# Constants made on GpSimd, columns turned by TensorE, and late constants moved off the weight queue, in a two-layer hybrid decoder

## The chip, the cores and the metric

The kernel runs on one core of a Trainium2 chip. The metric is device time in microseconds (us) of one execution. Three runs of the kernel before took 957.54, 958.25 and 959.33 us; the median, 958.25 us, is the time to compare with. One more execution was profiled; its span, from the first to the last instruction, is 955.9 us.

Engine names: TensorE (PE in the rows; PEld is its weight load), VectorE (DVE), ScalarE (ACT), GpSimd (POOL) and SyncE (SP, which issues most DMAs).

## The reference

Two layers of a decoder trunk, 256 tokens of width 1024, all in float32. What touches the change:

```python
for layer in range(2):
    h = rms_norm(x, norm_mix_pre[layer])
    m = mixer_block(h, positions, w_in[layer], conv_w[layer], ret_gn_w[layer], gla_w_a2[layer],
                    gla_b_a[layer], gla_gn_w[layer], w_branch_a[layer], w_branch_b[layer],
                    w_branch_c[layer], w_out[layer])
    x = x + rms_norm(m, norm_mix_post[layer])
    h = rms_norm(x, norm_ffn_pre[layer])
    f = (silu(h @ w_gate) * (h @ w_up)) @ w_down
    x = x + rms_norm(f, norm_ffn_post[layer])
```

`mixer_block` projects h with w_in (1024 x 8208, the first weights to be used) and cuts the result into the inputs of three branches and their gates: a short causal convolution of three taps (`conv_w`), a retention with rotary positions (cos and sin of position times frequency, masks of powers of a decay), and gated linear attention (GLA), whose decay comes from the data through a 16-column projection and `gla_w_a2`, `gla_b_a`. The branches' results are normalized per head (`ret_gn_w`, `gla_gn_w`), gated, projected and summed.

## The kernel before

**Products.** Float32 products are made of three products of two float32r parts: each operand is split into hi (a cast on ScalarE, `whi`, L206) and lo (the rest, a subtraction on VectorE, `wlo`, L208). TensorE then does hi hi, hi lo and lo hi into one bank (`piece`, L290). The activations are split in the same way into `hT0hi`, `hT0lo` for the first 128 tokens (tile 0) and `hT1hi`, `hT1lo` for the second (tile 1).

**The weight stream.** `Weights` lists all weights in the order of use, cut in units of at most 128 x 1024 numbers, 512 KB. A unit is loaded by SP into one of four buffers `raw` (L192), split into one of eight slots, and multiplied with both tiles. A load waits for a free `raw`, which the subtraction of an earlier unit gives back; a split waits for a slot, which TensorE's last product of an earlier unit gives back. In the first layer the units are, in order: 0 to 4 the GLA q and k (512 columns), 5 and 6 half of the GLA output gate (256 columns), 7 to 9 the other half with the 16 decay columns (272 columns), 10 to 13 the retention q (`rq`), 14 to 17 its k (`rk`), 18 to 21 its v, and so on.

**What sets the order.** TensorE's and SP's programs run in the order that the code writes, in which `Order` interleaves side tasks (generators that yield a time or a condition) with the stream of products. ScalarE, VectorE and GpSimd get an order from the tile scheduler, which follows priorities (`urgent()`, `tc.high_priority`) and `issue_after` bounds. Each engine runs its instructions strictly in that order, and so do the DMA queues' issuing engines: an instruction that waits holds up all behind it.

**The start.** TensorE multiplies zeros (`warm`) until data is there. `first_norm` transposes x through `ident` (L296), multiplies by the norm's weight column `wcol` (L539) and splits; the norm's factor per token is applied later, when a bank is drained (`drain`, L577, with `rs` as scale). `first_rstd` makes these factors: a sum of squares on ScalarE (L547), then on GpSimd an addition (L548) and a power (L370).

**Constants.** One table `consts` in DRAM holds the identity, two decay masks for the retention (`cst`, C_DD and C_DO), `mlev` (nine 128x128 matrices that sum log decays within blocks of 1 to 64 tokens), `lmask` (seven 128x64 masks) and the rotary frequencies. SP loads them: the identity first of all (L317), `freq` and `posi` (L322, L323) ahead of the first weights, `lmask` and the decay masks (L364, L365) behind unit 7; GpSimd's queue loads `mlev` (L552). At each layer's start SP loads the two head-norm weights broadcast to all partitions (`gnw`, L564), the decay projection (`wa`, L569, L570) and the conv taps as columns (`cw`, L573, three DMAs).

**The two places that drain.** The bank of the 272-column block is drained by four instructions (L577, into `ga` and `long`); the next products of tile 1 need these banks. `ga` is transposed and copied to `gaT` (L658), and `wa` times `gaT` (names `ac<-wa,gaT`) is in TensorE's program right behind.

## Time and profile before

| | |
|---|---|
| median of three runs | 958.25 us (957.54 to 959.33) |
| span of the profiled execution | 955.9 us |
| mean granted TensorE clock | 0.986 |
| TensorE busy | 927.0 us (97%) |
| VectorE busy | 578.2 us (60%) |
| ScalarE busy | 461.6 us (48%) |
| GpSimd busy | 74.4 us (8%) |
| DMA | 166.55 MB, mean 174 GB/s |

Busy shares are means over the whole span. In a timeline row the bracket at the end gives the idle time of the engine just ahead of the instruction and what ended it. `x3` is a count. A granted clock of 1.00 is 2.4 GHz, 0.5 is 1.2 GHz. The executions' own time is some 2 us above the span, which begins with the first instruction.

### The profile page before, as it was taken

How to read it: one execution, taken by the hardware profiler on the slowest of the kernel's cores; microseconds unless marked ns; L12 is line 12 of the kernel's file. 1: busy time of each engine (PE TensorE's matmuls, PEld its weight loads, DVE VectorE, ACT ScalarE, POOL GpSimd, SP SyncE). 2: the span in 40 equal slices, each digit the busy share in tenths (PEclk: the TensorE clock that was granted, in tenths of full speed). 3: DMA queues.
4: the chain of work that ended last, by engine and by line, in shares of the span. 5: the costliest groups of instructions: out<-in, count | busy, mean ns of one | idle time of the engine just before them, and what ended most of it. 6: DMA issues, size and time to landing. Idle time of an engine off the chain costs nothing.

```text
span 955.9 us, 12593 instructions
## 1 busy us (share of the span) xinstructions
PE 927.0 (97%) x4828; PEld 755.9 (79%) x4828; DVE 578.2 (60%) x830; ACT 461.6 (48%) x609; POOL 74.4 (8%) x83
## 2 busy tenths in 40 slices
PE   7779999999999999999989999999999999999997
PEld 5757888888888888888977778888888888888895
DVE  5569858654467655455475976775456765455443
ACT  4465364544436644444456545454444564444431
POOL 1002220101000000000010233010020000000000
PEclk8889999999999999999999999999999999999999
DMA  9994558877635766655779546697765467566521
GB/s 188 192 235 133 130 140 178 239 191 180 198 110 177 242 179 202 215 184 189 155 93 214 160 114 129 178 237 180 188 187 169 139 211 209 182 211 180 188 96 45
DMA packets 94240, 166.55 MB, mean 174 GB/s; under 512 B 9922, under 2 KB 19428, under 8 KB 94180
## 3 DMA queue, kind: packets, MB, share of 16 engines
q1 hardware_dynamic: 94036, 165.16, 65.2%
q8 instruction: 38, 0.62, 0.3%
q0 software_dynamic: 144, 0.59, 0.2%
q14 instruction: 22, 0.18, 0.0%
HBM read 164.68 MB, written 1.05 MB: 173 GB/s over the span
## 4 chain that ended last, share of the span: by engine, by line
PE 83%; DMA 8%; DVE 4%; ACT 2%; issue 2%; POOL 1%; SPq 0%; POOLq 0%; DVEq 0%; ACTq 0%
PE mm L290 61%; PE ac L290 18%; DMA raw<-in_w_in_dram 8%; PE tp L296 3%; DVE wlo L208 2%; ACT whi L206 1%; POOL gt L795 1%; DVE yTlo L734 1%; DVE yThi L735 0%; DVE S L718 0%; DVE x L440 0%; DVE gt L793 0%; DVE gt L790 0%; DVE gt L504 0%; SPq L192 0%
## 5 line engine op out<-in xcount | busy, mean ns | idle before, releaser
L208 DVE TENSOR_TENSOR wlo<-raw,whi 128x1024 fp32r<-128x1024 f32 (+2 forms) x303 | 370.1, 1227 | 300.6 <-ACT whi L206 300.0
L206 ACT CAST whi<-raw 128x1024 fp32r<-128x1024 f32 (+2 forms) x303 | 314.7, 1040 | 354.5 <-PE mm L290 235.0
L290 PE MATMUL mm<-whi,hT0hi 128*128 128x512 f32 (+2 forms) x464 | 179.8, 388 | 2.6 <-ACT whi L206 2.6
L290 PE MATMUL mm<-whi,hT1hi 128*128 128x512 f32 (+2 forms) x464 | 180.2, 388 | 1.9 <-ACT long L577 1.9
L290 PE MATMUL mm<-whi,hT0lo 128*128 128x512 f32 (+2 forms) x464 | 177.2, 382 | 0.0
L290 PE MATMUL mm<-wlo,hT0hi 128*128 128x512 f32 (+2 forms) x464 | 177.0, 382 | 0.2
L290 PE MATMUL mm<-whi,hT1lo 128*128 128x512 f32 (+2 forms) x464 | 177.0, 381 | 0.0
L290 PE MATMUL mm<-wlo,hT1hi 128*128 128x512 f32 (+2 forms) x464 | 176.7, 382 | 0.0
L290 PEld LDWEIGHTS mm<-whi,hT0hi 128*128 128x128 f32 x464 | 88.8, 191 | 21.3 <-ACT whi L206 3.9
L290 PEld LDWEIGHTS mm<-whi,hT1hi 128*128 128x128 f32 x464 | 88.1, 190 | 20.4 <-ACT long L577 2.7
L290 PEld LDWEIGHTS mm<-wlo,hT0hi 128*128 128x128 f32 x464 | 88.7, 192 | 18.3 <-DVE wlo L208 1.7
L290 PEld LDWEIGHTS mm<-whi,hT1lo 128*128 128x128 f32 x464 | 87.6, 189 | 18.5 <-DVE hT1lo L404 0.5
L290 PEld LDWEIGHTS mm<-whi,hT0lo 128*128 128x128 f32 x464 | 88.7, 191 | 16.8
L290 PEld LDWEIGHTS mm<-wlo,hT1hi 128*128 128x128 f32 x464 | 87.8, 189 | 16.3
L290 PE MATMUL ac<-whi,yThi 128*128 128x512 f32 x176 | 71.3, 405 | 0.0
L290 PE MATMUL ac<-whi,yTlo 128*128 128x512 f32 x176 | 69.5, 395 | 0.0
L290 PE MATMUL ac<-wlo,yThi 128*128 128x512 f32 x176 | 69.4, 394 | 0.0
L370 POOL TENSOR_TENSOR rs<-rs,mhalf 128x1 f32<-128x1 f32 (+1 forms) x24 | 17.2, 716 | 442.6 <-DVE rs L432 441.3
L290 PEld LDWEIGHTS ac<-whi,yTlo 128*128 128x128 f32 x176 | 33.1, 188 | 7.7
L290 PEld LDWEIGHTS ac<-wlo,yThi 128*128 128x128 f32 x176 | 33.2, 189 | 6.7
L290 PEld LDWEIGHTS ac<-whi,yThi 128*128 128x128 f32 x176 | 33.2, 189 | 6.7
L290 PE MATMUL mm<-whi,yThi 128*128 128x512 f32 x96 | 38.2, 398 | 0.0
(154 smaller groups left out, 870.6 us busy)
## 6 DMA issues: line engine op xcount, KB each, us to landing
raw<-in_w_in_dram SPq DMA_DIRECT2D x123, 512.0 KB, 5.0
raw<-in_w_ffn_gate_dram SPq DMA_DIRECT2D x44, 512.0 KB, 3.7
raw<-in_w_ffn_up_dram SPq DMA_DIRECT2D x44, 512.0 KB, 3.7
raw<-in_w_ffn_down_dram SPq DMA_DIRECT2D x44, 512.0 KB, 3.6
raw<-in_w_out_dram SPq DMA_DIRECT2D x16, 512.0 KB, 3.8
raw<-in_w_branch_a_dram SPq DMA_DIRECT2D x8, 512.0 KB, 7.6
raw<-in_w_branch_b_dram SPq DMA_DIRECT2D x8, 512.0 KB, 4.2
raw<-in_w_branch_c_dram SPq DMA_DIRECT2D x8, 512.0 KB, 4.3
```

The costliest lines, as they stand in the source:

```text
L206: nc.scalar.copy(hi[:, c], raw[:, c])
L208: nc.vector.tensor_tensor(lo[:, c], raw[:, c], hi[:, c].bitcast(F32), ALU.subtract)
L290: T.matmul(acc, lhsT, rhs, start=start, stop=stop)
L296: T.transpose(acc, src, ident)
L370: return G.tensor_tensor(v, v, mhalf[:, :n], ALU.pow)
L734: V.tensor_tensor(h4(a), h4(f), qkT[t][:, pr, :].unsqueeze(1).to_broadcast([P, 4, P]), ALU.mult)
L795: G.tensor_tensor(a, a, b, ALU.add)
```

## The change

The program computes the same thing. What moves:

- The identity, `mlev` and `lmask` are made on GpSimd from memsets and `affine_select` (two for the identity, 44 for the others) and leave the constants table, which keeps the decay masks and the frequencies.
- The first norm's weight is loaded as eight rows and turned to columns by TensorE (`turned`), likewise the conv taps as twelve rows, once per layer.
- The first weight unit, `freq` and `posi` are issued by ScalarE; x comes first on SP; `wa` and the conv rows are issued by GpSimd.
- The decay masks are loaded by GpSimd between the two rotary additions of q, the head-norm weights behind those of k.
- The first units are split where `first_norm` says so (`hold`, `W.split()`), the trigonometry starts behind a split of tile 1's first half, and T1 goes from 1.4 to 2.0.

```diff
-PUMP0 = 4
-T1 = 1.4
+T1 = 2.0
-C_ID, C_DD, C_DO, C_M, C_LM, C_IF, C_END = 0, 128, 640, 1152, 2304, 2752, 2816
+C_DD, C_DO, C_IF, C_END = 0, 512, 1024, 1088
...
+    def keep(ap, pattern, base, row, fill=0.0):
+        G.affine_select(ap, ap.bitcast(F32), pattern, ALU.is_ge, fill, base, row)
+
+    for c in range(2):
+        nc.sync.dma_start(out=x_sb[0][:, c * 512:(c + 1) * 512], in_=ins["x"][0, 0:P, c * 512:(c + 1) * 512])
+    nc.scalar.dma_start(out=w_row, in_=ins["norm_mix_pre"][0].rearrange("(k p) -> k p", p=P))
     with tc.high_priority():
         V.memset(idle, 0.0)
+        G.memset(ident, 1.0)
+        keep(ident, [[1, P]], 0, -1)
+        keep(ident, [[-1, P]], 0, 1)
+        G.memset(one, 1.0)
+        G.memset(mhalf, -0.5)
         for t in TS:
             G.memset(gaT[t], 1.0)
-        nc.sync.dma_start(out=cst[:, C_ID:C_DD], in_=ins["consts"][:, C_ID:C_DD])
-        for c in range(2):
-            nc.sync.dma_start(out=x_sb[0][:, c * 512:(c + 1) * 512], in_=ins["x"][0, 0:P, c * 512:(c + 1) * 512])
-            if c == 0:
-                nc.sync.dma_start(out=w_col, in_=ins["norm_mix_pre"][0].rearrange("(k p) -> p k", p=P))
-        nc.sync.dma_start(out=freq, in_=ins["consts"][:, C_IF:C_END])
-        nc.sync.dma_start(out=posi, in_=ins["positions"][0].rearrange("(t p) -> p t", p=P))
...
-    for u in range(NRAW):
+    W.load(nc.scalar)
+    A.preload_act_table_set("exp_and_others")
+    for u in range(1, NRAW):
         if u == X1_AT:
             nc.sync.dma_start(out=x_sb[1], in_=ins["x"][0, P:2 * P, :])
         W.load()
-    W.pump(PUMP0)
-    nc.sync.dma_start(out=flat(lmask), in_=ins["consts"][:, C_LM:C_IF])
-    nc.sync.dma_start(out=cst[:, C_DD:], in_=ins["consts"][:, C_DD:C_M])
+    nc.scalar.dma_start(out=freq, in_=ins["consts"][:, C_IF:C_END])
+    nc.scalar.dma_start(out=posi, in_=ins["positions"][0].rearrange("(t p) -> p t", p=P))
+
+    def level_constants():
+        G.memset(flat(mlev).bitcast(F32), 1.0 / 16.0)
+        G.memset(flat(lmask), 1.0)
+        for l in reversed(range(7)):
+            b = 1 << l
+            n = P // (2 * b)
+            early, late = [mlev[:, 1 + l, :].rearrange("p (n s b) -> p n s b", s=2, b=b)[:, :, s, :] for s in range(2)]
+            keep(late, [[-2 * b, n], [0, b]], -b, 1)
+            keep(late, [[2 * b, n], [1, b]], b, -1)
+            keep(early, [[-2 * b, n], [-1, b]], -1, 1)
+            keep(early, [[2 * b, n], [0, b]], b - 1, -1)
+            m = lmask[:, l, :].rearrange("p (n b) -> p n b", b=b)
+            keep(m, [[-2 * b, n], [0, b]], 0, 1)
+            keep(m, [[2 * b, n], [0, b]], b - 1, -1)
+        keep(mlev[:, 0, :], [[-1, P]], -1, 1)
+        keep(mlev[:, 8, :], [[1, P]], 0, -1)
...
         yield TRIG0
         posf = small("posf", NT)
-        V.tensor_copy(posf, posi)
+        with tc.issue_after(first_split[1][1][1].ins):
+            V.tensor_copy(posf, posi)
...
+    def turned(row, n, o):
+        yield O.acquire("tp")
+        tp = bank("tp")
+        T.transpose(tp[:, :n], row, ident[:n, :n])
+        A.copy(o, tp[:, :n])
+        O.release("tp", 1, 1.0)
...
             O.release("ac", 1, 1.6)
+            W.urgent = list(last[-1])
+            W.split()
+        W.hold = 1 - t
...
-            last = rsqrt(rs)
+            rsqrt(rs)
             rstd[t] = rs
-        with tc.issue_after(last.ins):
-            G.dma_start(out=flat(mlev), in_=ins["consts"][:, C_M:C_LM])
 
     warm(N_W0)
+    level_constants()
+    O.finish(O.add(turned(w_row, 8, w_col)))
...
-            nc.sync.dma_start(out=w, in_=ins[nme][l].partition_broadcast(P))
+            G.dma_start(out=w, in_=ins[nme][l].partition_broadcast(P))
...
-        gla_w, ret_w = gn_w("gla_gn_w"), gn_w("ret_gn_w")
-        nc.sync.dma_start(out=wa[0:16, :], in_=ins["gla_w_a2"][l])
-        nc.sync.dma_start(out=wa[16:17, :], in_=ins["gla_b_a"][l].rearrange("(o n) -> o n", o=1))
-        cw = p1.tile([P, 4, 3], F32, tag="cw", name=nm("cw"))
-        for i in range(3):
-            nc.sync.dma_start(out=cw[:, :, i], in_=ins["conv_w"][l, i].rearrange("(c p) -> p c", p=P))
+        G.dma_start(out=wa[0:16, :], in_=ins["gla_w_a2"][l])
+        G.dma_start(out=wa[16:17, :], in_=ins["gla_b_a"][l].rearrange("(o n) -> o n", o=1))
+        cw_row = ut()[:12, :P]
+        G.dma_start(out=cw_row, in_=ins["conv_w"][l].rearrange("i (c p) -> (i c) p", p=P))
+        cw = p1.tile([P, 3, 4], F32, tag="cw", name=nm("cw"))
...
-            G.tensor_tensor(a, a, b, ALU.add)
+            last = G.tensor_tensor(a, a, b, ALU.add)
+            with tc.issue_after(last.ins):
+                if (t, into is rqT) == (0, True):
+                    if l == 0:
+                        G.dma_start(out=cst, in_=ins["consts"][:, C_DD:C_IF])
+                    O.add(turned(cw_row, 12, flat(cw)))
+                elif (t, into is rkT) == (1, True):
+                    gn.extend([gn_w("gla_gn_w"), gn_w("ret_gn_w")])
```

How this moves instructions, at three places. Names carry a buffer number behind an underscore where rows would read alike.

**GpSimd, start of the program.** Before: four memsets, the pool's configuration (ISA), the two factors `rs` of the first norm, and the load of `mlev`.

```order
L314 MEMSET gaT_82 17x128
L314 MEMSET gaT_83 17x128
L315 MEMSET one 128x1
L316 MEMSET mhalf 128x4
L548 ISA
L548 TENSOR_SCALAR rs_276<-ss_275 128x1
L370 TENSOR_TENSOR rs_276<-rs_276,mhalf 128x1
L548 TENSOR_SCALAR rs_282<-ss_281 128x1
L370 TENSOR_TENSOR rs_282<-rs_282,mhalf 128x1
L552 DMA mlev<-in_consts_dram 128x1152
```

The changed kernel begins with the identity:

```order
L304 MEMSET ident 128x128
L307 MEMSET one 128x1
L308 MEMSET mhalf 128x4
L310 MEMSET gaT_84 17x128
L297 ISA
L297 AFFINE_SELECT ident<-ident 128x128
L310 MEMSET gaT_85 17x128
L297 AFFINE_SELECT ident<-ident 128x128
L358 MEMSET mlev 128x1152
L359 MEMSET lmask 128x448
L297 AFFINE_SELECT mlev<-mlev 128x64 x2
```

and after the last of the 44 selects for `mlev` and `lmask` goes on:

```order
L297 AFFINE_SELECT mlev<-mlev 128x128 x2
L587 DMA wa_203<-in_gla_w_a_dram 16x256
L588 DMA wa_203<-in_gla_b_a_dram 1x16x16
L590 DMA ut_206<-in_conv_w_dram 12x128
L567 TENSOR_SCALAR rs_322<-ss_321 128x1
L377 TENSOR_TENSOR rs_322<-rs_322,mhalf 128x1
L567 TENSOR_SCALAR rs_328<-ss_327 128x1
L377 TENSOR_TENSOR rs_328<-rs_328,mhalf 128x1
```

The configuration has moved ahead of the identity, and the factors `rs` behind all selects and three DMAs; the load of `mlev` is gone.

**SP, around units 7 to 9.** Before, in front of and behind the constants:

```order
L192 DMA raw6_125<-in_w_in_dram 128x4x256
L192 DMA raw7_131<-in_w_in_dram 128x3x272
L364 DMA lmask_99<-in_consts_dram 128x448
L365 DMA cst_77<-in_consts_dram 128x1024
L564 DMA gnw_10_164<-in_gla_gn_w_dram 128x512
L564 DMA gnw_11_166<-in_ret_gn_w_dram 128x512
L569 DMA wa_12_168<-in_gla_w_a2_dram 16x256
L570 DMA wa_12_168<-in_gla_b_a_dram 1x256
L573 DMA cw_13_171<-in_conv_w_dram 128x4x1 x3
L192 DMA raw8_203<-in_w_in_dram 128x3x272
L192 DMA raw9_209<-in_w_in_dram 128x2x272
```

Now, the same units:

```order
L175 DMA raw6_231<-in_w_in_dram 128x4x256
L175 DMA raw7_246<-in_w_in_dram 128x3x272
L175 DMA raw8_252<-in_w_in_dram 128x3x272
L175 DMA raw9_258<-in_w_in_dram 128x2x272
L175 DMA raw10_268<-in_w_in_dram 128x2x512
L175 DMA raw11_274<-in_w_in_dram 128x2x512
```

Nothing stands between the units any more.

**ScalarE, the drains of the 272-column block and the first gaT copy.** Before, from the cast of unit 12 to the copy (`mm_43` and `mm_44` are the block's banks):

```order
L206 CAST whi12_337<-raw12_234 128x1024
L577 ACTIVATE ga_46_493<-mm_43_415,rs_23_276 128x16
L577 ACTIVATE long_36_357<-mm_43_415,rs_23_276 128x256
L577 ACTIVATE ga_47_496<-mm_44_416,rs_26_282 128x16
L577 ACTIVATE long_42_413<-mm_44_416,rs_26_282 128x256
L206 CAST whi13_385<-raw13_249 128x1024
L206 CAST whi14_407<-raw14_267 128x1024
L206 CAST whi15_441<-raw15_300 128x1024
L206 CAST whi16_469<-raw16_341 128x1024
L206 CAST whi17_487<-raw17_389 128x1024
L206 CAST whi18_517<-raw18_411 128x1024
L658 COPY gaT0_82<-tp_52_580 16x128
```

Now, the drains (`mm_44`, `mm_45`), from the same cast on:

```order
L189 CAST whi12_382<-raw12_286 128x1024
L189 CAST whi13_430<-raw13_295 128x1024
L595 ACTIVATE long_43_458<-mm_38_404,rs_27_328 128x256
L189 CAST whi14_452<-raw14_313 128x1024
L189 CAST whi15_486<-raw15_345 128x1024
L189 CAST whi16_514<-raw16_386 128x1024
L595 ACTIVATE ga_47_538<-mm_44_460,rs_24_322 128x16
L595 ACTIVATE long_37_402<-mm_44_460,rs_24_322 128x256
L595 ACTIVATE ga_48_541<-mm_45_461,rs_27_328 128x16
L595 ACTIVATE long_43_458<-mm_45_461,rs_27_328 128x256
```

and the copy:

```order
L189 CAST whi17_532<-raw17_434 128x1024
L189 CAST whi18_562<-raw18_456 128x1024
L522 ACT_TABLE_LOAD
L522 ACTIVATE sin_620<-gt_34_373 128x2x64
L521 ACTIVATE cos_619<-gt_52_598 128x128
L189 CAST whi19_586<-raw19_490 128x1024
L480 ACT_TABLE_LOAD
L189 CAST whi20_610<-raw20_518 128x1024
L676 COPY gaT0_84<-tp_53_625 16x128
L595 ACTIVATE ut_59_657<-mm_49_544,rs_24_322 128x512
L685 ACTIVATE gt_55_636<-ac_54_634 128x256
L676 COPY gaT1_85<-tp_58_645 16x128
```

The four drains have moved from behind the cast of unit 12 to behind that of unit 16, the copy gaT0 from behind unit 18 to behind unit 20; between the two copies there is no cast now, where before there was one.

## Rows read from the trace of the kernel before

**Rows 1.** The page: the span; TensorE's busy tenths in 40 slices.

```profile
span 955.9 us, 12593 instructions
PE   7779999999999999999989999999999999999997
```

**Rows 2.** Windows: stretch, length, PE PEld DVE ACT POOL busy, PEclk, DMA, GB/s.

```profile
20.00:30.00 10.00, 5.54 (x23) 4.09 (x23) 4.86 (x8) 4.08 (x5) 2.19 (x5) 0.95 1.04 231
...
60.00:70.00 10.00, 7.17 (x18) 4.67 (x19) 6.50 (x8) 6.48 (x12) 1.27 (x1) 0.66 1.01 211
70.00:80.00 10.00, 9.46 (x87) 7.36 (x86) 8.91 (x15) 6.87 (x13) 2.20 (x1) 1.00 0.64 192
sum 80.00, PE 63.50 PEld 48.91 DVE 49.83 ACT 43.63 POOL 6.39; mean PE 7.94 PEld 6.11 DVE 6.23 ACT 5.45 POOL 0.80
```

**Rows 3.** Chain of waits to 110 us: start, length, what held it.

```profile
20.01 10.02 DMA raw<-in_w_in_dram
```

**Rows 4.** DMA answer for 0 to 80 us: its total.

```profile
DMA packets 12230, 16.27 MB, mean 203 GB/s; under 512 B 3633, under 2 KB 5954, under 8 KB 12226
```

**Rows 5.** Timeline, DMA issues after 20 us: start, length, engine, line, operation, names.

```profile
20.43 0.48 SPq L364 DMA_DIRECT2D lmask<-in_consts_dram  x1
23.13 0.80 POOL L552 DMA_DIRECT2D mlev<-in_consts_dram  x1
27.41 3.86 SPq L573 DMA_DIRECT2D cw<-in_conv_w_dram  x3
31.96 4.03 SPq L192 DMA_DIRECT2D raw<-in_w_in_dram  x4
```

**Rows 6.** Timeline, unit 7's cast and TensorE behind the drain.

```profile
30.05 0.87 ACT L206 CAST whi<-raw 128x816 fp32r<-128x816 f32 x1 [3.32 <-DMA raw<-in_w_in_dram]
31.56 1.12 PE L296 MATMUL tp<-cst,ut 128*128 128x128 f32 x4 [5.90 <-ACT ut L577]
```

**Rows 7.** Timeline, TensorE behind the block's drains, and unit 16's cast.

```profile
49.92 0.50 PE L290 MATMUL mm<-whi,hT1hi 128*128 128x512 f32 x1 [1.32 <-ACT long L577]
54.99 1.05 ACT L206 CAST whi<-raw 128x1024 fp32r<-128x1024 f32 x1 [0.22 <-DMA raw<-in_w_in_dram]
```

**Rows 8.** Timeline, around the two copies gaT, to unit 20's cast.

```profile
61.51 0.25 ACT L658 COPY gaT<-tp 16x128 f32<-16x128 f32 x1
61.86 0.67 PE L290 MATMUL ac<-wa,gaT 17*128 17x256 f32 x2 [2.52 <-issue]
65.83 1.19 PE L290 MATMUL ac<-wa,gaT 17*128 17x256 f32 x2 [0.96 <-ACT gaT L658]
66.88 1.03 ACT L206 CAST whi<-raw 128x1024 fp32r<-128x1024 f32 x1
66.94 0.80 PE L290 MATMUL mm<-whi,hT0hi 128*128 128x512 f32 x1
```

**Rows 9.** Timeline, TensorE's first product with weights.

```profile
8.97 0.80 PE L290 MATMUL mm<-whi,hT0hi 128*128 128x512 f32 x1 [2.18 <-ACT whi L206]
```

**Rows 10.** GpSimd: a timeline row; groups by form (busy us, mean ns).

```profile
19.87 0.22 POOL L548 TENSOR_SCALAR rs<-ss 128x1 f32<-128x1 f32 x1 [18.73 <-ACT xs L547]
...
L370 POOL TENSOR_TENSOR rs<-rs,mhalf 128x1 f32<-128x1 f32 x16 | 8.9, 561 | 442.0 <-DVE rs L432 441.3
L745 POOL COPY glo<-yTlo 128x128 f32<-128x128 f32 x4 | 3.6, 924 | 8.1 <-DVE yTlo L734 8.1
L745 POOL COPY ghi<-yThi 128x128 f32<-128x128 f32 x4 | 1.4, 365 | 40.5 <-ACT ut L577 34.3 <-DVE yThi L735 6.2
```

**Rows 11.** Timeline, VectorE's rotary products; the second runs beside one of GpSimd.

```profile
65.87 0.68 DVE L790 TENSOR_TENSOR gt<-ut,cos 128x512 f32<-128x512 f32 x1
67.47 1.67 DVE L790 TENSOR_TENSOR gt<-ut,cos 128x512 f32<-128x512 f32 x1
```

**Rows 12.** Timeline, TensorE at the second layer's start.

```profile
517.92 0.50 PE L290 MATMUL mm<-whi,hT1hi 128*128 128x512 f32 x1 [0.55 <-ACT long L577]
523.81 0.48 PE L290 MATMUL ac<-wa,gaT 17*128 17x256 f32 x1 [1.18 <-ACT gaT L658]
```

More of the change, by code (lines that the diff above doesn't have):

```diff
@@ L172, in __init__ @@
         self.units, self.blocks, self.live, self.raw = [], [], {}, {}
-        self.loaded, self.issued, self.freed, self.next, self.hold = 0, 0, 0, 0, 0
+        self.loaded, self.issued, self.freed, self.next, self.hold = 0, 0, 0, 0, 1
     def add(self, ap2d, r0, nk, c0, n):
@@ L185, in add, with load @@
         self.blocks.append(us)
-    def load(self):
+    def load(self, queue=None):
         if self.loaded == len(self.units) or self.loaded == self.issued + NRAW:
@@ L191, in load @@
         raw = self.raw_pool.tile([P, UW], F32, tag="raw", name=f"raw{self.loaded}")
-        self.nc.sync.dma_start(out=raw[:, :nk * n].rearrange("p (k n) -> p k n", n=n),
+        (queue or self.nc.sync).dma_start(out=raw[:, :nk * n].rearrange("p (k n) -> p k n", n=n),
                                in_=w[r0:r0 + nk * P, c0:c0 + n].rearrange("(k p) n -> p k n", p=P))
```

32 lines of the change are left out of this document (8 added, 24 removed).

## The prediction

> **What bounds the kernel now.** The page's slices come first: of the 40, TensorE is busy over 90% in all but the first three (72 us) and the last [rows 1], so the change can win little where TensorE does not wait, and it waits at the start. The windows of ten microseconds say how much. In the first 80 us it is busy 63.50 us [rows 2], so 16.5 us are idle; in two of the eight windows it is worst, 5.54 us busy from 20 to 30 us, and 7.17 us at a granted clock of 0.66 from 60 to 70 us [rows 2]. A mean of 0.66 between 1.0 and 0.5 (2.4 and 1.2 GHz) is some 6.8 us at the lower level (the last of it at 66.94, where a product takes 0.80 us instead of 0.50, [rows 7, 8]), which costs about 3.4 us of TensorE's time there.
>
> Next the DMA answer for the same stretch: 16.27 MB at 203 GB/s [rows 4], with the DMA engines' share at 1.04 and 1.01 in those two windows [rows 2]. So the start is paced by the weight stream, and what else rides in it counts. Then the chain of waits: one piece, 10.02 us from 20.01 us, is the load of weight unit 7 alone [rows 3]. The issue rows say why: behind that load SP issues lmask at 20.43, then the decay masks, the two norm weights and the twelve-column conv taps, three instructions that end at 31.27, GpSimd adds mlev at 23.13, and the next weight unit is issued at 31.96 [rows 5]. All of these transfers share the stream with unit 7.
>
> Last, which wait ends last on TensorE. At 31.56 it has idled 5.90 us, released by the drain of the first bank (ut) on ScalarE, which stood behind the cast of unit 7, and that cast had waited 3.32 us for the DMA [rows 6]. At 49.92 it has idled 1.32 us, for the drains that free the banks of the 272-column block [rows 7]. At 61.86 and at 65.83 it waits for the copies gaT (2.52 and 0.96 us), the first of which stands behind the cast of unit 18 [rows 8]. So the pattern is: a DMA feeds a cast, ScalarE works in program order, and what TensorE needs stands behind that cast.
>
> **What goes out of the stream.** By the tile shapes, times four bytes: the identity 0.066 MB, lmask 0.229 MB and mlev 0.590 MB are no longer loaded; the decay masks (0.524 MB) and the two norm weights (2 x 0.262 MB) are loaded after the rotary additions, so behind the weights of this stretch. That is 1.93 MB, at 203 GB/s [rows 4] 9.5 us of stream. Late in the stretch they come at a time when the DMA share is falling (0.64 from 70 to 80 us, [rows 2]), so I cost their new place at nothing; if that cover were gone they would cost 1.05 MB, or 5 us of stream, but beside a TensorE that has its units. The column loads of 1024 and 1536 four-byte pieces become rows of 512 bytes; I count that within the rounding of the rest. On SP the weight unit after unit 7 no longer stands behind eight other issues. I take a lead of the weight stream of 7 us out of the 9.5 (bounds 4 and 9.5), because a unit's load also waits for a free raw buffer, and those come free only as fast as ScalarE and VectorE split.
>
> A rule of the Trainium skill speaks against one part: "DMA: Bandwidth & Descriptors", section "Issuing engines are not separate DMA queues", says that issuing from several engines saves only the issuing time. By it the loads moved to ScalarE's and GpSimd's queues would win nothing but issue slots, and the lead would be that of the removed bytes and of the program order alone; the sum here already counts only those.
>
> **What the new order gives back.** The order of ScalarE's instructions has moved. The drains of the 272-column block now stand behind the cast of unit 16, where they stood behind that of unit 12; the first gaT copy stands behind unit 20, where it stood behind unit 18. TensorE needs both. Unit 16 was cast at 54.99 [rows 7]; 7 us earlier is 48.0, plus 1.05 for the cast and about 0.7 for the drains ahead of the last one, makes 49.7, against 49.92 before: nothing won. Unit 20 was cast at 66.88 [rows 8]; 7 us earlier is 59.9, plus 1.03 for the cast and 0.35 from the copy's start to TensorE (61.51 to 61.86, [rows 8]), makes about 61.3, against 61.86: 0.5 won. Each microsecond of lead more or less moves both by as much. So the 5.90 us of idle at 31.56 get shorter, but TensorE meets the next wait earlier and sits there longer.
>
> What stays won lies behind that. Units 19 and 20 are split by then and no cast stands between the two copies, so the second gaT wait of 0.96 us [rows 8] goes, and with units 21 and 22 early the 0.54 us that TensorE still idles from 70 to 80 us [rows 2]: 1.5 us. Of the 3.4 us that the low clock costs there I take half, 1.7 us (bounds 0 and 3.4): the clock fell after an idle stretch, and one such stretch, before the first gaT product, remains.
>
> **What is added.** TensorE turns the norm row before it can start, and ScalarE copies it, one transpose and one small copy: 0.6 us, from the copy gaT (0.25 us, 0.35 from its start to the product that needs it, [rows 8]) and the like of 0.25 for the transpose; the conv rows add one transpose per layer where TensorE is full, 0.1 us each. Tile 1's transposes stand behind three more products; those products were waiting anyway. VectorE's angle work stands behind unit 5's split now, and the sine after it; its first user is the rotary product at 65.87 us [rows 11], so I cost it at nothing. The second layer's start loses 0.55 and 1.18 us in the same two places [rows 12]; half a megabyte leaves its stream, but the same order stands there, so I take 0 of it (bounds 0 and 1.7).
>
> Sum: 0.5 + 1.5 + 1.7 - 0.6 - 0.2 = 2.9 us. The profiled span is 955.9 us [rows 1]; the median of the runs is 958.25, 2.35 us around it. 958.25 - 2.9 = **955.4 us**.
>
> **GpSimd's new work, which is the risk.** GpSimd now makes the identity (a memset, two AFFINE_SELECTs of 128x128), then two large memsets, 42 selects of 64 columns and two of 128, issues three DMAs, and only then computes the two factors of the first norm, which the first drain needs. No row of before shows a select. From below: 0.22 us, what an operation of one column took [rows 10]. From above: a 128x128 copy beside a busy VectorE took 0.924 us and an undisturbed one 0.365 [rows 10], so 64 columns with 0.22 fixed are 0.29 to 0.57 us. I take 0.33, nearer to the undisturbed copy, with a small wait between dependent pairs. Then: 1.1 us where GpSimd is free, 0.8 for the identity, 1.4 for the memsets, 44 x 0.33 = 14.5, three issues at 0.80 [rows 5] = 2.4: 20.2 us, and 0.22 + 0.56 [rows 10] for the factor, so 21 us, ahead of the drain, which is wanted at about 26 (the cast ahead of it is done near 31 in [rows 6], less part of the lead). Hidden. At 0.57 the end is 31.5 us, later than that of today; a delay begins at (26 - 6.5) / 44 = 0.44 us, where 6.5 are the other terms, and each 0.1 us more is 4.4 us.
>
> The other cost is the pool's configuration instruction: it now stands ahead of the first select, so ahead of the identity, and thereby of every transpose. In before it stands just ahead of the first factor's operation, which comes after 18.73 us of waiting for ScalarE [rows 10], so anything up to that would have been hidden and no row prices it. The first product starts at 8.97 us after 2.18 us of idle that the first weights caused [rows 9]: some 2 us of delay of the identity are free. The Trainium skill, "GPSIMD Engine Reference", section 2.1 "Instruction dispatch", says that the first call of freshly loaded pool code pays about 6 us that no instruction shows. By that page the identity would come at 8 us, the first products at 11 and the factor at 27 us, which is case (b) below; no run here shows it yet.
>
> **The rivals.** (a) *The full lead reaches TensorE*: if the drains find their banks free in time, all of 7 us less 0.8 arrives, some 952 us. Against it stand the two moved positions in ScalarE's order. 0.08.
> (b) *The lead is half of what I think*: the identity late by more than 2 us, so casts behind hT0hi late, raw buffers late, lead 4 us. Then unit 16's drains end at 52.7 (2.8 us later than today) and gaT at 64.3 (2.4 later), while 1.5 and up to 3.4 us come back: 957 to 959.5, no change. It is also where the change does not do what it says: the bytes leave, and nothing starts earlier. 0.22.
> (c) *Slower: the factor of the first norm is late.* One mechanism: ScalarE's drain waits for GpSimd, and behind it in order the casts of units 8, 9 and all later ones, so the stream stops too. It decides from a factor ready at about 30 us: a select of 0.53 us, or less by 0.02 us (1/44) for each microsecond that the identity is late. Also, VectorE slows beside GpSimd: a 128x512 product took 1.67 us beside one of GpSimd's and 0.68 without [rows 11]; the splits between 3 and 20 us would share that. At 0.57 us and an identity late by 5 us (within the 18.73 that hide it in [rows 10]) the factor is there at 36.5, 5 us after TensorE goes on today [rows 6]; of that 0 to 2 us come back as above: 961 to 963 us. 0.25.
>
> **How the numbers follow.** My own case, a lead of 6 to 9.5 us: 953 to 956.3, 0.45. Faster by over 0.2% (1.9 us, about what runs of this kernel can tell apart) has the forecast and (a), 0.52 with what lies on the edge; within 0.2% (b), 0.23; slower (c), 0.25. The range takes in (a) to its middle and the lower half of (c): 950.5 to 962.
>
> **What would show it.** Right: no weight issue later than about 24 us for unit 8; the 5.9 us idle on TensorE shorter by some 4 us; a new wait of some 5 us that ends near 50 us behind the cast of unit 16; the gaT product near 61 us; clock at 1.0 in most of 60 to 70 us; selects of 0.25 to 0.4 us, the first factor before 26 us. Wrong: a select over 0.45 us, a gap between the configuration and the first select of over 3 us, the first drain released by GpSimd, or the wait near 50 us gone, which would be case (a).

## The result and the profile after

Four runs of the changed kernel took 947.40, 947.54, 948.13 and 951.51 us, median **947.84 us**; four of the kernel before, taken beside them, 957.54 to 959.53, median 958.79. The ratio is 0.9894 with an interval of 0.9875 to 0.9914: faster by 10.9 us, where 2.9 were forecast. The time lies below the stated range (950.5). The profiled execution took 948.13 us; its span is 946.4 against 955.9 us. These two spans differ by 9.5 us, 1.4 less than the medians do, and everything below accounts for the spans.

The page after, beside [rows 1]: the span, and TensorE's busy tenths in 40 slices. They differ by one tenth in the second and third slice, and nowhere else: the view of the whole is too coarse for this change.

```profile
span 946.4 us, 12659 instructions
PE   7889999999999999999989999999999999999997
```

The windows after, with the columns of [rows 2]:

```profile
20.00:30.00 10.00, 5.12 (x24) 4.60 (x23) 4.72 (x10) 3.90 (x6) 5.73 (x12) 0.78 1.01 139
...
60.00:70.00 10.00, 8.74 (x43) 6.46 (x45) 9.99 (x14) 7.05 (x15) 5.31 (x5) 1.00 0.73 221
70.00:80.00 10.00, 10.00 (x118) 8.11 (x117) 9.51 (x29) 4.54 (x7) 2.34 (x3) 1.00 0.38 107
sum 80.00, PE 66.16 PEld 52.52 DVE 59.23 ACT 47.12 POOL 32.94; mean PE 8.27 PEld 6.57 DVE 7.40 ACT 5.89 POOL 4.12
```

TensorE is busy 66.16 us of the first 80 instead of 63.50, only 2.66 more. The rest is in the clock: 60 to 70 us now run at 1.00, where they ran at 0.66. Before, the clock stood at 0.50 from 8.5 to 15.3, from 29.0 to 35.8 and from 63.1 to 69.9 us; after, only from 25.7 to 32.5. The windows of these stretches, three before and one after:

```profile
8.50:15.30 6.80, 5.68 (x16) 4.05 (x17) 4.92 (x13) 2.42 (x4) 0.00 (x0) 0.50 1.03 186
29.00:35.80 6.80, 4.24 (x17) 3.95 (x18) 4.44 (x14) 2.11 (x4) 0.00 (x0) 0.50 0.86 192
63.10:69.90 6.80, 5.84 (x14) 3.72 (x13) 5.17 (x7) 5.18 (x10) 1.27 (x1) 0.50 1.00 226
```

```profile
25.70:32.50 6.80, 5.69 (x21) 5.11 (x22) 3.07 (x6) 3.38 (x7) 0.36 (x1) 0.50 0.94 199
```

If the busy time in them is counted at half, the first 80 us hold 55.6 us of work at the full clock before and 63.3 after, 7.7 us more. So a reader who counts only idle time on TensorE sees a third of the gain.

What TensorE waits for up to 80 us: the kernel after, then the kernel before (engine, line, operation, awaited; us in total, times, longest).

```profile
PE tp L279 <- ACT ut L595: 4.9, 1, 4.9
PE ac L273 <- ACT gaT L676: 2.6, 1, 2.6
...
PE ac L273 <- DVE glo L690: 1.3, 1, 1.3
PE mm L273 <- ACT whi L189: 1.1, 1, 1.1
PE mm L273 <- ACT hT1hi L410: 1.0, 1, 1.0
PE mm L273 <- ACT long L595: 0.8, 1, 0.8
```

```profile
PE tp L296 <- ACT ut L577: 5.9, 1, 5.9
PE mm L290 <- ACT whi L206: 2.6, 2, 2.2
PE ac L290 <- issue: 2.5, 1, 2.5
...
PE mm L290 <- ACT long L577: 1.3, 1, 1.3
PE ac L290 <- ACT gaT L658: 1.0, 1, 1.0
```

The largest waits, for the first drain and for gaT, keep their names and nearly their lengths; each comes earlier. The one for the first bank's drain ends at 26.81 instead of 31.56 [rows 6], the one for the 272-column drains at 45.36 instead of 49.92 [rows 7], the first gaT product starts at 57.38 instead of 61.86, the second at 59.61 without a wait instead of 65.83 [rows 8]. A new one of 1.26 us, for VectorE's glo, ends at 64.81. The timelines of TensorE, of ScalarE's casts of units 7, 16 and 20 and its first drain, and of SP's issue of unit 8:

```profile
26.81 1.12 PE L279 MATMUL tp<-ident,ut 128*128 128x128 f32 x4 [4.88 <-ACT ut L595]
45.36 0.50 PE L273 MATMUL mm<-whi,hT1hi 128*128 128x512 f32 x1 [0.77 <-ACT long L595]
57.38 0.69 PE L273 MATMUL ac<-wa,gaT 17*128 17x256 f32 x2 [2.58 <-ACT gaT L676]
59.61 0.69 PE L273 MATMUL ac<-wa,gaT 17*128 17x256 f32 x2
64.81 0.50 PE L273 MATMUL ac<-mlev,glo 128*128 128x512 f32 x1 [1.26 <-DVE glo L690]
```

```profile
25.30 0.87 ACT L189 CAST whi<-raw 128x816 fp32r<-128x816 f32 x1 [2.21 <-DMA raw<-in_w_in_dram]
26.08 0.68 ACT L595 ACTIVATE ut<-mm,rs 128x512 f32<-128x512 f32 x1
43.72 1.05 ACT L189 CAST whi<-raw 128x1024 fp32r<-128x1024 f32 x1 [0.49 <-DVE wlo L191]
56.13 1.04 ACT L189 CAST whi<-raw 128x1024 fp32r<-128x1024 f32 x1 [0.64 <-DMA raw<-in_w_in_dram]
```

```profile
18.74 0.37 SPq L175 DMA_DIRECT2D raw<-in_w_in_dram  x1
```

Unit 16's cast stood at 54.99 [rows 7] and unit 20's at 66.88 [rows 8]: 11.27 and 10.75 us of lead, not 7. The first 80 us still move 15.95 MB at 199 GB/s (16.27 at 203 in [rows 4]): the same rate, with more weights and less else.

GpSimd's work, some of its instructions (timeline):

```profile
0.80 0.20 POOL L304 MEMSET ident<- 128x128 f32 x1 [0.29 <-POOLq L1083]
1.25 0.28 POOL L297 TENSOR_SCALAR_AFFINE_SELECT ident<-ident 128x128 f32<-128x128 f32 x1
...
3.71 0.23 POOL L297 TENSOR_SCALAR_AFFINE_SELECT lmask<-lmask 128x64 f32<-128x64 f32 x1
...
13.03 1.52 POOL L297 TENSOR_SCALAR_AFFINE_SELECT lmask<-lmask 128x64 f32<-128x64 f32 x1
...
21.76 0.56 POOL L297 TENSOR_SCALAR_AFFINE_SELECT mlev<-mlev 128x128 fp32r<-128x128 f32 x2
...
24.52 0.58 POOL L377 TENSOR_TENSOR rs<-rs,mhalf 128x1 f32<-128x1 f32 x1
```

The factor that the first drain needs is there at 25.10; the drain starts at 26.08, as soon as unit 7's cast is done. The cover was 1.0 us.

### The profile page after: what moved, and what is told of

It reads as the page before. It is cut to its first block, busy times and chain, and to the rows that moved or that the text cites. A ratio compares the mean times of both kernels' runs of the same rounds, so it can differ in the third digit from the quotient of the medians.

```text
span 946.4 us, 12659 instructions
## 1 busy us (share of the span) xinstructions
PE 922.2 (97%) x4831; PEld 753.9 (80%) x4831; DVE 580.0 (61%) x830; ACT 462.1 (49%) x612; POOL 100.2 (11%) x142
## 3 DMA queue, kind: packets, MB, share of 16 engines
HBM read 163.79 MB, written 1.05 MB: 174 GB/s over the span
## 4 chain that ended last, share of the span: by engine, by line
PE 87%; DMA 5%; DVE 5%; issue 2%; ACT 1%; POOL 1%; POOLq 0%; DVEq 0%; ACTq 0%
PE mm L273 65%; PE ac L273 19%; DMA raw<-in_w_in_dram 5%; PE tp L279 3%; DVE wlo L191 2%; POOL gt L813 1%; ACT whi L189 1%; DVE yTlo L752 0%; DVE yThi L753 0%; DVE S L736 0%; DVE gt L811 0%; DVE x L447 0%; DVE gt L808 0%; DVE glo L690 0%; POOL rs L377 0%
```

## The experiments

Where a part has its cost is read best from one quantity: the start of ScalarE's cast of each weight unit. The tables give it in us, one profiled execution per kernel. before_cw_row is the kernel before with one thing changed, the other variants in the first table are the kernel after with one thing undone.

| unit | before | after | start_before | masks_loaded | consts_on_sp | wcol_pieces | issue_by_sp | before_cw_row | taps_pieces |
|---|---|---|---|---|---|---|---|---|---|
| 7 | 30.05 | 25.30 | 30.13 | 26.15 | 24.20 | 29.54 | 26.68 | 29.76 | 22.89 |
| 10 | 43.60 | 32.24 | 37.81 | 36.98 | 33.72 | 34.69 | 34.46 | 42.65 | 33.29 |
| 16 | 54.99 | 43.72 | 48.84 | 48.22 | 46.08 | 47.05 | 45.97 | 54.03 | 46.75 |
| 20 | 66.88 | 56.13 | 61.47 | 57.72 | 57.83 | 58.70 | 57.22 | 67.58 | 59.60 |
| 24 | 81.23 | 73.73 | 79.07 | 75.74 | 75.87 | 76.72 | 74.80 | 84.69 | 77.18 |

| unit | ident_loaded | t1_14 | layer1_on_sp | layer1_pieces |
|---|---|---|---|---|
| 16 | 46.99 | 45.33 | 45.15 | 44.33 |
| 20 | 57.50 | 56.63 | 56.09 | 57.01 |
| 24 | 75.51 | 75.75 | 73.67 | 76.14 |

From unit 24 on TensorE is full and the shift stays what it is to the end of layer 0, so that row is what a kernel gains or loses in that layer. How far one profile can be trusted, the last two columns say: layer1_on_sp and layer1_pieces change layer 1 only, and up to 64 us their engines run the same instructions in the same order as the kernel after. Their units still differ from its units by up to 1.4 us at unit 16, 0.9 at unit 20 and 2.4 at unit 24. The last figure belongs to a stretch at half clock from 59.3 to 66.1 us in layer1_pieces, which the other two do not have. A difference in unit 24 of some 2 us is thus within what the clock alone can make, and unit 20, ahead of that stretch, is the safer row. At unit 20 the start (5.34), the taps' pieces (3.47) and the norm column's pieces (2.57) stand clear; masks_loaded (1.59), consts_on_sp (1.70), ident_loaded (1.37) and issue_by_sp (1.09) lie little above 0.9, and t1_14 (0.50) lies within it.

Medians are of four runs unless said otherwise, and ratios are to runs of the kernel before taken beside them; the kernel after has 0.9894 [0.9875, 0.9914]. A kernel now and then has a run some 3 us longer (951.51 above), so that a median's difference below 2 us is weak by itself. The intervals of masks_loaded, consts_on_sp, issue_by_sp, ident_loaded and t1_14 overlap that of the kernel after, and that of wcol_pieces just does.

**start_before.** The old start: identity loaded, the norm column as 1024 four-byte pieces, frequencies, positions and the first weights issued by SP, tile 1's transposes three products earlier.

```diff
...
+    nc.sync.dma_start(out=ident, in_=ins["consts"][:, C_ID:C_END])
...
+            nc.sync.dma_start(out=w_col, in_=ins["norm_mix_pre"][0].rearrange("(k p) -> p k", p=P))
+    nc.sync.dma_start(out=freq, in_=ins["consts"][:, C_IF:C_M])
+    nc.sync.dma_start(out=posi, in_=ins["positions"][0].rearrange("(t p) -> p t", p=P))
...
-    W.load(nc.scalar)
...
+    W.load()
...
```

> The changed kernel with the start of the kernel before: identity loaded first, norm column by four-byte pieces, frequencies and positions ahead of the first weights on SP, T1 1.4; masks still made by GpSimd, late constants still late. Theory 'stream': the start gave 1.4 us of the lead at unit 0 and some more by unit 7; unit 8 and later 1.5 to 4 us later, time 949 to 952 us. Rival 'start': nearly the whole gain of the first layer (7.5 us) goes: 954 to 956 us.

Measured 954.59 us (six runs, 952.75 to 956.77), ratio 0.9958 [0.9940, 0.9977]. Unit 7 is 4.83 us late, unit 24 5.34. The rival 'start' named the time rightly. So about half of the gain of 9.5 us goes with the start, which the prediction had held for next to nothing.

**wcol_pieces.** Only the norm column again as 1024 pieces, on ScalarE's queue.

```diff
-    nc.scalar.dma_start(out=w_row, in_=ins["norm_mix_pre"][0].rearrange("(k p) -> k p", p=P))
+    nc.scalar.dma_start(out=w_col, in_=ins["norm_mix_pre"][0].rearrange("(k p) -> p k", p=P))
...
-    O.finish(O.add(turned(w_row, 8, w_col)))
```

> The changed kernel, but the norm column is loaded by 1024 four-byte pieces again, from the same queue and place as its row; TensorE turns nothing there. Theory 'pieces': such pieces keep the 16 DMA engines busy far beyond their 4 KB; in the run with the old start the stream moved 180 GB/s from 0 to 10 us against 222. Then units 1 to 7 are cast 2 to 4 us later and the time is 950 to 952.5 us. Rival 'issue order': the old start lost its time by the places of the identity, frequencies and first unit on SP's queue, and the pieces cost below 0.5 us: 947.5 to 948.5 us.

Measured 951.08 us, 0.9923 [0.9903, 0.9943], within the range of 'pieces'; unit 20 is 2.57 us late, unit 24 2.99 (with a stretch at half clock from 60.2 to 63.6 us in between). The windows of this kernel, then of the kernel after (columns of [rows 2]):

```profile
0.00:10.00 10.00, 7.16 (x22) 4.38 (x23) 4.39 (x7) 3.54 (x5) 9.34 (x37) 1.00 0.86 209
10.00:20.00 10.00, 8.22 (x34) 5.16 (x32) 6.06 (x7) 4.28 (x5) 10.00 (x18) 1.00 1.01 204
20.00:30.00 10.00, 3.43 (x14) 2.48 (x14) 4.10 (x10) 4.65 (x7) 5.33 (x11) 0.80 1.04 110
```

```profile
0.00:10.00 10.00, 6.90 (x23) 4.56 (x24) 4.45 (x7) 3.63 (x6) 9.34 (x37) 1.00 0.84 222
10.00:20.00 10.00, 8.75 (x39) 6.38 (x38) 7.41 (x9) 6.43 (x9) 10.00 (x17) 1.00 1.02 220
```

The DMA engines are as busy in both, but move 209, 204 and 110 GB/s instead of 222, 220 and 139 [the third is in the windows above], 0.58 MB less in 30 us. The pieces are 4 KB in all. The records of the packets give 9 ns to each, 0.6 us for 1024 over 16 engines, so their own time does not explain 2.6 us. Nor do these windows show how they slow the rest: ident_loaded, which has no such pieces, moves 0.45 MB less in the same 30 us (218, 204 and 114 GB/s) and is 1.37 us late. That the column as pieces costs time is shown; by what path is not.

**issue_by_sp.** Frequencies, positions and the first weights issued by SP again.

```diff
-    W.load(nc.scalar)
...
+    W.load()
...
-    nc.scalar.dma_start(out=freq, in_=ins["consts"][:, C_IF:C_END])
-    nc.scalar.dma_start(out=posi, in_=ins["positions"][0].rearrange("(t p) -> p t", p=P))
```

> The changed kernel, but frequencies, positions and unit 0 are issued by SP behind x, ahead of units 1 to 3; ScalarE issues only the norm row. Theory 'pieces': units 0 to 3 are issued some 1 us later each, which the DMA engines, full from 2 us on, swallow: 947.5 to 949 us. Rival 'issue order': 950 to 952.5 us.

Measured 949.89 us, 0.9915 [0.9891, 0.9939], between the two ranges; unit 24 is 1.07 us late. The rule that the prediction named, from the Trainium skill's "DMA: Bandwidth & Descriptors" ("Issuing engines are not separate DMA queues"), is not contradicted here: what is saved is of the size of issuing time. At the start it may count in full: unit 0 is cast at 7.83 us instead of 6.87, and unit 20 is 1.09 us late, though that is little more than two profiles of one program differ by.

**ident_loaded** and **t1_14.** The two remaining parts of the start, each alone: the identity from memory, and the old place of tile 1's transposes.

```diff
-T1 = 2.0
+T1 = 1.4
```

> The kernel after with the identity loaded by SP as its first transfer instead of made by GpSimd. Theory A (the load is 0.066 MB and one issue ahead of all others on SP, so x and the weights behind it come later): casts of units 0 to 8 later by 0.7 to 1.3 us, median 948.6 to 949.3. Theory B (the identity is small and TensorE waits for x and the first weights later than for it): within 0.3 us of 947.9.

> The kernel after with the old 1.4 for the time of tile 1's transposes in the order of TensorE's program: they stand three products earlier. Theory A (the order of the start matters by itself: it is part of the 1.3 us of the old start's 5.35 that neither the column pieces, 2.99, nor the issues on SP, 1.08, explain): casts of units 3 to 8 later by 0.3 to 1.3 us and the median 948.2 to 949.2. Theory B (those products wait for weights anyway): within 0.3 us of 947.9.

Measured 949.01 us (0.9905 [0.9889, 0.9922], unit 24 1.78 late) and 949.79 us (0.991 [0.9896, 0.9925], unit 24 2.02 late). The first lies within what theory A gave for it, the second 0.6 us above. In t1_14 nearly all of the 2.02 us comes with the clock: unit 20 is 0.50 late, then the clock stands at 0.50 from 58.8 to 65.6 us. So T1 is not shown to be worth anything. The four parts alone make 2.57 + 1.09 + 1.37 + 0.50 = 5.53 us at unit 20, where all together make 5.34; at unit 24 it is 7.86 against 5.34, at unit 16 10.46 against 5.12. The start as a whole is shown; of its parts only the column pieces stand clear.

**masks_loaded.** lmask and mlev loaded again, as before; no selects but the identity's.

```diff
-    level_constants()
...
+            nc.sync.dma_start(out=flat(lmask), in_=ins["consts"][:, C_LM:C_ID])
...
+        with tc.issue_after(last.ins):
+            G.dma_start(out=flat(mlev), in_=ins["consts"][:, C_M:C_LM])
```

> The changed kernel with one part undone: lmask and mlev are loaded again (lmask by SP behind unit 7, mlev by GpSimd behind the norm's factors), no selects for them. Theory 'stream': the gain is the lead of the weight stream, paid out one for one where TensorE waits for a drain or gaT behind a cast. 0.82 MB more at some 215 GB/s is 3.8 us: unit 16 and 20 cast 3.5 to 5 us later than in the changed kernel (43.7 and 56.1), time 951 to 953 us. Rival 'start': the gain was made in the first 20 us, where TensorE ran at the full clock; these loads lie behind it: 947 to 949 us.

Measured 950.31 us, 0.9915 [0.9888, 0.9942], between the two ranges. Unit 10 is 4.74 us late, which is 0.82 MB at 203 GB/s (4.0 us) and a little, and unit 16 4.50, as 'stream' said; unit 20 is only 1.59 late, which it did not say, and at unit 24 2.01 are left. What TensorE waits for up to 80 us in it:

```profile
PE tp L295 <- ACT ut L594: 9.9, 2, 5.4
```

The second drain is a wait too now (4.5 us beside 5.4), and part of what is lost there comes back by unit 24, as later waits fall away.

**consts_on_sp.** The decay masks and the two norm weights of layer 0 (1.05 MB) back on SP behind unit 7.

```diff
...
+            nc.sync.dma_start(out=cst, in_=ins["consts"][:, C_DD:C_IF])
+            for nme in ("gla_gn_w", "ret_gn_w"):
...
+                nc.sync.dma_start(out=gn0[-1], in_=ins[nme][0].partition_broadcast(P))
```

> The changed kernel with one part undone in the first layer: the decay masks and the two head-norm weights are issued by SP behind unit 7 again. Theory 'stream': 1.05 MB at 215 GB/s is 4.9 us, and unit 8's load stands behind three issues: units 8 to 20 cast 4.5 to 7 us later, time 952 to 955 us. Rival 'start': 947 to 949 us.

Measured 950.85 us, 0.9921 [0.9896, 0.9946], between the two ranges; unit 10 is 1.48 us late, unit 16 2.36, unit 24 2.14. 1.05 MB is 5.2 us of stream at 203 GB/s, so this part was priced too high.

**selects_twice.** The selects of the masks made twice.

```diff
-        for l in reversed(range(7)):
+        for l in list(reversed(range(7))) * 2:
...
```

> The changed kernel with the 44 selects of mlev and lmask made twice (the second pass changes nothing). In the changed kernel they took from 3.3 to 22.3 us, and the first norm factor was ready at 25.1, just ahead of the drain at 26.08. Theory 'factor late': the second pass ends at 35 to 42 us, the first drain and all casts behind it wait for GpSimd: 10 us or more of the lead go, 955 to 962 us. Rival 'covered': TensorE meets a later wait anyway, 948 to 951 us.

Measured 958.62 us (ten runs, 958.03 to 959.75), 1.0000 [0.9989, 1.0010]: the whole gain is gone. The timelines of GpSimd and ScalarE, and what TensorE waits for:

```profile
39.55 0.57 POOL L378 TENSOR_TENSOR rs<-rs,mhalf 128x1 f32<-128x1 f32 x1
```

```profile
40.16 0.69 ACT L596 ACTIVATE ut<-mm,rs 128x512 f32<-128x512 f32 x1 [13.26 <-POOL rs L378]
```

```profile
PE tp L279 <- ACT ut L596: 19.0, 1, 19.0
```

The factor comes at 40.12, 15.0 us later (44 more selects at 0.34 us); ScalarE's drain waits 13.26 us for it, and with it all later casts. Rival (c) is a real mechanism, and 1.0 us was all that kept this kernel from it.

**factors_first** and **drain_early.** Two attempts at a kernel faster than the one after: the factors ahead of the masks on GpSimd; and, on top, the first drain ahead of the casts of units 6 and 7.

```diff
+        with tc.issue_after(last.ins):
+            level_constants()
...
-    level_constants()
```

The lines of drain_early that put the drain first:

```diff
+                d = drain(qk, acc, t)
+                if l == 0 and t == 0:
+                    W.urgent[0] = d
```

> The changed kernel with GpSimd's order turned: the first norm's two factors ahead of the memsets and selects of mlev and lmask, which then run from about 22 to 42 us. Theory 'covered': the factor was ready at 25.1 us, the cast ahead of the drain ends at 26.1, so nothing is won: 947.3 to 948.6 us. Rival: the selects slow VectorE between 3 and 22 us, and the first units come earlier without them: 945.5 to 947 us.

> As factors_first, and the first drain is put ahead of the casts of units 6 and 7 (splits are looked ahead by 3 units until the 272-column block is drained). TensorE should go on at about 23 us instead of 26.8. Theory 'next wait': the drains behind unit 15 or 16 and gaT behind unit 20 stay, TensorE reaches them earlier and waits longer: 947 to 948.5 us. Rival: what it waits less at 26.8 is won in the end: 943.5 to 945.5 us.

Measured 949.32 us (0.9910 [0.9885, 0.9936]) and 949.33 us (0.9902 [0.9887, 0.9917]): nothing won, each a little above the range of its theory. In the second the wait for the first drain is gone, and TensorE goes on at 22.67 us. But the drain of the second tile, which ScalarE does behind the casts of units 8 and 9, is now waited for 4.91 us; gaT follows with 3.6, unit 20 is cast at 56.26 us (56.13 in the kernel after), and the clock falls again from 56.9 to 67.2. The timeline of TensorE at the two drains, then the window of the low clock:

```profile
22.67 0.60 PE L279 MATMUL tp<-ident,ut 128*128 128x128 f32 x4
...
32.45 1.11 PE L279 MATMUL tp<-ident,ut 128*128 128x128 f32 x4 [4.91 <-ACT ut L596]
```

```profile
60.00:70.00 10.00, 10.00 (x30) 7.19 (x30) 6.56 (x10) 6.09 (x12) 4.92 (x5) 0.64 0.54 174
```

**layer1_on_sp** and **layer1_pieces.** In layer 1, norm weights, wa and conv rows back on SP at the layer's start; then the same with the conv taps as three loads of 512 pieces there.

```diff
+        if l == 1:
+            for w, nme in zip(gn1, ("gla_gn_w", "ret_gn_w")):
+                nc.sync.dma_start(out=w, in_=ins[nme][l].partition_broadcast(P))
+        q = nc.sync if l == 1 else G
...
+            for i in range(3):
+                nc.sync.dma_start(out=cw[:, i, :], in_=ins["conv_w"][l, i].rearrange("(c p) -> p c", p=P))
```

> The changed kernel with one part undone in the second layer only: head-norm weights, decay projection and conv rows are issued by SP at that layer's start. Theory 'stream': the 1.95 us that the changed kernel wins between units 150 and 180 go away, the first layer stays: 949.3 to 950.3 us. Rival: those 1.95 us come from the order of the other engines there, and it stays at 947.5 to 948.3 us.

> The changed kernel, but the second layer's head-norm weights, decay projection and conv taps are issued by SP at that layer's start, and the taps as 3 x 512 four-byte pieces as before; it differs from the run layer1_on_sp only in these pieces. Theory 'pieces': they take the 1.95 us that the changed kernel wins in the second layer, which layer1_on_sp did not: 949.5 to 950.5 us. Rival: those 1.95 us come from ScalarE's order in that layer: as layer1_on_sp, 947.5 to 948.5 us.

Measured 948.18 us (0.9898 [0.9870, 0.9926]), as its rival said, and 952.60 us (0.9939 [0.9917, 0.9961]), above both ranges. From the cast of unit 24 of layer 0 to the end of the span it is 874.7 us in the kernel before, 872.7 in the kernel after, 872.6 in layer1_on_sp and 875.7 in layer1_pieces. So moving the half megabyte late is worth nothing in layer 1, and with the pieces its gain is gone. Of their 3.0 us some 1.6 are there by unit 19 of layer 1; most of the rest comes with a stretch at half clock from 520.1 to 523.5 us, which layer1_on_sp does not have. SP also issues for longer: 2.67 us for the three loads, 1.14 for the row. The windows of the layer's start, each from 3.0 us behind the issue of the first norm weight; with pieces and without:

```profile
484.60:504.60 20.00, 17.33 (x100) 14.98 (x99) 10.22 (x13) 10.06 (x15) 0.79 (x2) 0.91 1.00 161
```

```profile
482.00:502.00 20.00, 17.21 (x98) 15.05 (x97) 11.08 (x13) 10.12 (x16) 0.79 (x2) 0.91 1.00 187
```

The same DMA share, 161 GB/s instead of 187. (The rest of this median's difference is the stretch at half clock in layer 0, from 59.3 to 66.1 us, as far as the one profile shows it.)

**before_cw_row**, **taps_pieces** and **posi_turned.** Do pieces cost wherever they stand? First the kernel before with layer 0's conv taps as one row; then the kernel after with those taps as pieces again, on SP behind unit 7; then the kernel after with the positions (256 pieces) as rows too.

```diff
-        for i in range(3):
-            nc.sync.dma_start(out=cw[:, :, i], in_=ins["conv_w"][l, i].rearrange("(c p) -> p c", p=P))
...
+            nc.sync.dma_start(out=cw_row, in_=ins["conv_w"][l].rearrange("i (c p) -> (i c) p", p=P))
```

> The kernel before with one part of the change alone, in the first layer only: the conv taps are loaded as twelve rows by one DMA at the same place on SP and turned by TensorE, instead of 3 x 512 four-byte pieces. Theory 'pieces': 1536 pieces cost 1.5 times what 1024 did for the norm column (2.99 us), so 4 us of stream behind unit 7, and SP's three issues (27.41 to 31.27) shrink: units 8 to 16 are cast 3.5 to 5 us earlier, time 954 to 956 us. Rival 'bytes': the constants' 1.9 MB set that stretch and the pieces hide beside them: 957.5 to 959 us.

> The kernel after, with the conv taps of layer 0 loaded as three column loads of 512 four-byte pieces each on SP, behind the weight unit 7, where the kernel before had them; the row and its turn by TensorE are left out in layer 0, all else keeps its order nearly. Theory (four-byte pieces slow the stream that runs beside them wherever they stand, as 1024 of them cost 2.99 us at the start and 1536 some 2.7 us in layer 1): the casts from unit 8 on come 2 to 4.5 us later, and the median is 950 to 952.4. Rival (they cost only where the stream has nothing to spare behind them; the run with the taps as one row in the kernel before won only 0.6 us at unit 8): unit 8 later by 0 to 0.7 us, median within 1 us of 947.9.

> The changed kernel with its last column load, the positions (256 four-byte pieces), loaded as two rows and turned by TensorE. Theory 'pieces': a quarter of the norm column's 2.99 us, 0.75 us of stream ahead of unit 2: units 4 to 20 are cast some 0.7 us earlier, time 946.6 to 947.5 us. Rival: with so few pieces the stream does not feel them: 947.6 to 948.5 us.

before_cw_row took 962.79 us, 1.0047 [1.0029, 1.0064], slower than before, which no theory expected. Unit 8 came only 0.6 us earlier and unit 16 0.96, and the first copy gaT now stood behind the cast of unit 19 instead of 18, so that the gaT product at 66.13 had waited 4.91 us:

```profile
66.13 1.19 PE L290 MATMUL ac<-wa,gaT 17*128 17x256 f32 x2 [4.91 <-issue]
```

In the kernel before, beside the constants, the taps' pieces are thus not shown to cost more than 1 us of the casts. taps_pieces puts them into the kernel after and keeps the order nearly: 955.33 us (ten runs, 952.50 to 957.22), 0.9966 [0.9952, 0.9979], above both ranges. In the profile of its fastest run unit 8 is not late (29.02 us), unit 10 is 1.05 late, unit 20 3.47 and unit 24 3.45; SP issues unit 8 at 20.23 instead of 18.74, behind the three loads. Its window beside that of the kernel after, 139 GB/s, above (122 to 139 in the three kernels with one layer 0):

```profile
20.00:30.00 10.00, 5.44 (x26) 4.83 (x25) 6.29 (x15) 5.42 (x9) 6.56 (x10) 0.77 0.94 94
```

So 1536 pieces with their issues on SP cost 3.5 us there. Most of its runs are 2.7 to 4.7 us longer still, which the one profile does not explain. posi_turned, 948.64 us (0.9895 [0.9878, 0.9911]), 0.1 above the range of its rival, wins nothing: no cost of 256 pieces shows, though TensorE waited 3.9 us for the conversion of the row, which could hide a small one.

## Why the prediction was wrong, by its steps

**What bounds the kernel** held: the weight stream paces the first 75 us, the gain lies there (7.50 of the 9.5 us of span by unit 24), and TensorE's waits stand behind casts in ScalarE's order.

**The formula for what the order gives back** held to a few tenths. Unit 16's cast less the lead, plus 1.75, is 54.99 - 11.27 + 1.75 = 45.47; measured 45.36. Unit 20's, 66.88 - 10.75 + 1.38 = 57.51; measured 57.38. So the two places gave 4.6 and 4.5 us, where 0 and 0.5 were forecast from a lead of 7.

**The lead is the step that failed.** 7 us, with 9.5 as an upper end; 11.27 measured at unit 16 and 10.75 at unit 20, and at least 9.8 in all three kernels with the layer 0 of the kernel after. The upper end was bytes over rate, and so had no room for causes that are not bytes. With the parts undone one at a time, unit 16 moves by 5.12 (the start), 4.50 (the masks) and 2.36 us (the late constants), 12.0 together for 11.27. Of the 9.5 the masks' 4.0 were about right, the late constants' 5.2 twice too much, and the start, which bytes price at 0.3, was missing. In it stood the column pieces ("within the rounding of the rest": 2.57 us at unit 20) and perhaps SP's issues, which the prediction counted for unit 8 only (1.09 us). The taps' pieces were in the same phrase; what they cost in the kernel before is open.

**With the lead as measured, the sum comes out.** The first gaT product comes 4.48 us earlier instead of 0.5. From there to unit 24 another 3.02 us are won: 2.9 from the clock (busy 5.84 us at 0.50 from 63.1 to 69.9 us before, past the 66.94 where the prediction read the last of it, and none at 0.50 here), where 1.7 were forecast; 0.23 of idle time, since the 0.96 and 0.54 us went as forecast but the wait for glo, 1.26 us, is new; less 0.1 for the turn of the conv rows. Together 7.50. The 0.6 us for turning the norm row is part of the measured lead and is not taken off again. That the clock gave back all is luck: layer1_pieces, with the same layer 0, has a stretch at half clock from 59.3 to 66.1 us and gains 5.09 us by unit 24. "The clock falls after an idle stretch, and one remains" was no argument: 2.58 us of idle before gaT were followed by a granted clock of 1.00 here, and 2.52 us before [rows 8] by 0.50.

**Layer 1** was taken as 0, bounds 0 and 1.7; it gave 2.0 us (9.5 in all less 7.50). The reason given for a gain, half a megabyte less, is not its cause: layer1_on_sp puts the bytes back and loses nothing. With the 1536 pieces back the gain is gone, the same term again.

**GpSimd's work** was nearly the end of it. A select of 64 columns took 0.23 us at its shortest, below the 0.29 that the prediction worked out, but up to 1.52, far over its 0.57; the 44 took 19.0 us from 3.32 to 22.3, 0.43 each with the next one's start, against a threshold of 0.44 that the prediction worked out and 0.33 that it took. The drain was wanted at 26.08 (the prediction said 26), so 4.1 of the 5 us of slack that it counted on were gone. That the doubled selects cost 10.1 us of span (956.5 against 946.4) bears out the mechanism of rival (c).

**The pool's code.** The Trainium skill, "GPSIMD Engine Reference", section 2.1 "Instruction dispatch", gives some 6 us for the first call of freshly loaded code. The trace shows no such gap ahead of these selects: the identity's memset starts at 0.80, its first select at 1.25 us. So the identity was not late, which case (b) needed.

**What would show it.** Unit 8's issue at 18.74 (24 at the latest: right); the first wait some 4 us shorter (1.0, though it ends 4.75 earlier: wrong); a wait of 5 us near 50 behind unit 16 (0.77 at 45.36: wrong, and that was to be read as case (a)); gaT near 61 (57.38: wrong); clock at 1.0 from 60 to 70 (right); selects of 0.25 to 0.4 (0.23 to 1.52: wrong); the factor before 26 (25.10: right). A select over 0.45 us was a sign of being wrong, and it came, but the cover of 1.0 us held. Case (a), the full lead less 0.8, did not happen either: of 11.27 us of lead 4.56 reached TensorE at the 272-column drains, and of 10.75 us 4.48 at gaT. The order took back what the formula says; the lead was larger.

## What to carry to other kernels

Bytes over rate gave no upper bound for this start-up stretch: the start, nearly without bytes, was worth 5.3 us here, more than the masks or the late constants. Load a per-partition column as rows and turn it, where there are a thousand pieces or more beside a stream that others wait for; 256 showed no cost here. Before a difference between two profiles is put down to a change, see how far two profiles of one program differ. When work moves to a free engine, compare its end with the moment it is wanted, at the disturbed duration, and write the slack down: 1.0 us here, on a chain that took 19.
